# Thirty-two bytes more in a small constant: the weight tiles and all tiles behind them move in SBUF, the activations do not

## The chip, the cores and the metric

The kernel runs on one core of a Trainium2 chip. The metric is the device time of one execution in microseconds. Three runs of the kernel before took 2510.86, 2509.39 and 2510.89 us, so the median is 2510.86 us.

## The reference, cut to what matters

Two layers of a decoder trunk work on 256 tokens of width 2048. In each layer the input is projected, a gated linear recurrence (HGRN2) and a sparse attention (NSA) run on the parts, and three more projections follow:

```python
h = x @ w_in[l]                                   # 2048 -> 6704 columns
y = concat(hgrn2(...), nsa(...)) @ w_out[l]       # 2048 -> 2048
x = layer_norm(DN_ALPHA * x + y, ...)
f = conv_ffn(x, w_up[l], conv_w, conv_b, w_down[l])   # 2048 -> 2*5632 -> 2048
x = layer_norm(DN_ALPHA * x + f, ...)
```

Every number is float32, and the weights, some 430 MB, are read from HBM once.

## The kernel before, in words

**The work.** A projection is cut into units of eight pairs. A unit is one weight block `raw` of 128x1024 floats that comes in by DMA (L281). ScalarE, or GpSimd for some blocks, rounds it to a high part `whi` (L237, L235), VectorE subtracts to get the low part `wlo` (L238), and TensorE then does eight pairs of matmuls in `units` (L300): a high one (L325, or L322 for the last output tile), in which `whi` is loaded as weights and 512 columns stream past (256 tokens in a high and a low part), and a low one (L328) with `wlo` and 256 columns. Each takes its 128x128 weights from columns `128*i` of the block. In `w_up` and `w_down` eight high matmuls go first and eight low ones after them (`group=8`); in `w_out` they alternate. What streams past is `x` in `w_in` and `w_up`, `o` in `w_out` and `f` in `w_down`.

Two projections go the other way round (`tok_units`, L347): there `x` is the weights and the block streams past (L363 to L365), 512 columns at a time in the value units `w_v`, and 280 in the units `w_vg`. A `w_vg` block holds two slices of 280 columns, the second 1120 bytes behind the first; in the built program three matmuls on the first slice and three on the second take turns.

**The order of the work.** SyncE alone issues the loads, up to seven units ahead. There are five `raw` buffers, four of `whi` and four of `wlo`. A load waits until VectorE has finished with the `raw` buffer, a split waits until TensorE has finished with the part buffer.

**Where the tiles lie.** Tiles of a pool are placed one behind the other in each partition, each size rounded up to 32 bytes. The pool of constants comes first (`setup`, L167, and `load_consts`, L180), then the pool of the weights, then those of the layer. The diff touches `lbt`, a scratch tile of eight numbers in each of six rows (L217), used once at the start. The built program of before has these starts, in bytes of a partition:

| tile | start | past a multiple of 64 |
|---|---|---|
| `x` (32768 bytes) | 16512 | 0 |
| `par` | 49280 | 0 |
| `cf32` (identity, rotation tables) | 52832 | 32 |
| `cb` | 55552 | 0 |
| `ones` | 56480 | 32 |
| `lbt`, `lb` | 57088, 57280 | 0 |
| `raw`, five of 4096 bytes | 57408 | 0 |
| `whi`, `wlo`, four of 4096 bytes each | 77888, 94272 | 0 |
| `o0` to `o7`; later `f` on the same bytes | 110720 | 0 |
| `kh`, `kl`, `v`, `hz`, `sg`, `q`, `vcmp`, P and PT tiles; `z`, `s1`, `sq`; `ch`, `ct` | 143488 on | 0 |
| `hv`, `hg` | 221024, 225120 | 32 |

The second slice of a `w_vg` block lies 1120 bytes into its tile, which is 32 past a multiple of 64. The slices of `sg` that are loaded as weights at L1132 are 240 bytes apart, so one in four of them starts on a multiple of 64.

Of the kernel before, what the change touches and what calls it, by code (L numbers as in the profile page):

```python
# [29 lines left out]
F32 = mybir.dt.float32  # L30
# [73 lines left out]
class Trunk:  # L104
# [75 lines left out]
    def load_consts(self):  # L180
        nc, cp, a = self.nc, self.cp, self.a

        def ld(name, shape, dt):
            t = self.t(cp, shape, dt, name)
            self.after(nc.sync.dma_start(t, a[name]), self.load)
            return t

        self.after(self.load_par(0), self.load)
        self.lbl = ld("lbl", [128, L, 8], F32)
        self.cf = ld("cf32", [128, 673], F32)  # L190
        self.ident32 = self.cf[:, 641:673]
        self.cb = self.t(cp, [128, 416], BF16, "cb")
        self.lm = self.t(cp, [128, 80], U8, "lm")
        raw = self.t(self.wp, [128, 1024], F32, "raw", bufs=RAW_BUFS)
        self.after(nc.sync.dma_start(raw[:, :496], a["masks"]), self.load)
        nc.vector.tensor_copy(self.cb, raw[:, :416])
        nc.vector.tensor_copy(self.lm, raw[:, 416:496])
        self.ident = self.cf[:, 0:128]
        self.rc = self.cf[:, 128:384]
        self.rs = self.cf[:, 384:640]  # L200
        self.any = self.cf[:, 640:641]
        self.identb = self.cb[:, 0:128]
        self.caus = self.cb[:, 144:400]
        self.mask0 = self.cb[:, 128:416]
        self.ones = self.t(cp, [128, 128], F32, "ones")
        nc.gpsimd.memset(self.ones, 1.0 / D)
        self.eps = self.t(cp, [128, 3], F32, "eps")
        self.zero = self.eps[:, 2:3]
        nc.gpsimd.memset(self.zero, 0.0)
        self.warm = self.t(cp, [128, 1], F32, "warm")  # L210
        nc.gpsimd.memset(self.eps[:, 0:1], LN_EPS)
        nc.gpsimd.memset(self.eps[:, 1:2], RMS_EPS)
        self.half = self.t(cp, [128, 4], F32, "half")
        nc.gpsimd.memset(self.half, -0.5)

        v = nc.vector
        t = self.t(cp, [128, 6, 8], F32, "lbt")  # L217
        lb = self.lb = self.t(cp, [128, L, 2, 8], F32, "lb")
        v.tensor_max(t[:, 0], self.lbl[:, 0], self.lbl[:, 1])
        v.tensor_sub(t[:, 1], self.lbl[:, 0], t[:, 0])  # L220
        v.tensor_sub(t[:, 2], self.lbl[:, 1], t[:, 0])
        nc.scalar.activation(t[:, 1:3], t[:, 1:3], AF.Exp)
        v.tensor_add(t[:, 3], t[:, 1], t[:, 2])
        v.reciprocal(t[:, 3], t[:, 3])
        v.tensor_mul(t[:, 4], t[:, 1], t[:, 3])
        v.tensor_mul(t[:, 5], t[:, 2], t[:, 3])
        v.tensor_sub(lb[:, 0, 0], t[:, 4], t[:, 4])
        v.tensor_add(lb[:, 1, 0], t[:, 4], t[:, 5])
        v.tensor_sub(lb[:, 1, 0], lb[:, 1, 0], t[:, 4])
        for l in range(L):  # L230
            v.tensor_scalar(lb[:, l, 1], lb[:, l, 0], -1.0, 1.0, op0=ALU.mult, op1=ALU.add)
# [1111 lines left out]
```

## Time and profile before

| | |
|---|---|
| median of 3 runs | 2510.86 us (2509.39 to 2510.89) |
| profiled execution, its own time | 2509.09 us |
| its span | 2507.3 us |
| TensorE busy | 2451.8 us, 98% of the span |
| weight loads busy (overlap with TensorE) | 2116.0 us, 84% |
| VectorE, ScalarE, GpSimd busy | 71%, 48%, 17% |
| DMA | 436.99 MB, mean 174 GB/s |

Busy time is the union of an engine's instructions; matmuls are pipelined, so that the mean duration of one is longer than the distance between two. The profiled execution's own time is its span and 1.8 us around it.

### The profile page before, as it was taken

What the parts mean: (1) busy time and instruction counts of PE and PEld (TensorE: products, weight loads), DVE (VectorE), ACT (ScalarE), POOL (GpSimd) and SP (SyncE); (2) the same over time, 40 slices, a digit from 0 to 9 for tenths busy, and PEclk for the clock granted to TensorE, in tenths of its full rate; (3) what the DMA queues carried; (4) which work ended last, traced back from release to release, by engine and by line L of the source; (5) the groups of instructions that cost most, each with busy time, mean ns of one, the idle gap of its engine ahead of it and who ended that gap; (6) DMA issues with size and microseconds to landing.
All of it is one profiled execution on the core that took longest, in us unless ns stands there. A gap on an engine that the chain in (4) does not pass through costs nothing.

```text
span 2507.3 us, 41290 instructions
## 1 busy us (share of the span) xinstructions
PE 2451.8 (98%) x15993; PEld 2116.0 (84%) x15993; DVE 1780.8 (71%) x2705; ACT 1196.0 (48%) x2189; POOL 428.0 (17%) x403
## 2 busy tenths in 40 slices
PE   8999999999999999999989999999999999999997
PEld 7788877888888888888878888788888888888887
DVE  7767876787777777555597678766977777775554
ACT  4144425465555555334331444354655555553443
POOL 0444551300000000001014445513000000000011
PEclk9999999999999999999999999999999999999999
DMA  6644343556666555566546443445556565566562
GB/s 236 213 155 142 119 145 124 184 163 193 192 193 190 190 192 192 187 193 193 160 155 204 159 135 124 139 134 177 174 190 192 192 191 189 192 187 197 181 201 101
DMA packets 122884, 436.99 MB, mean 174 GB/s; under 512 B 13760, under 2 KB 14528, under 8 KB 122688
## 3 DMA queue, kind: packets, MB, share of 16 engines
q1 hardware_dynamic: 122688, 434.35, 54.0%
q8 instruction: 126, 2.06, 0.3%
q14 instruction: 70, 0.57, 0.1%
HBM read 432.20 MB, written 2.10 MB: 173 GB/s over the span
## 4 chain that ended last, share of the span: by engine, by line
PE 86%; DVE 8%; issue 2%; POOL 1%; ACT 1%; DMA 1%; SPq 0%; ACTq 0%; POOLq 0%; DVEq 0%
PE pj L325 49%; PE pj L328 26%; DVE wlo L238 3%; PE pj L322 1%; PE t L325 1%; DVE rope L400 1%; PE pj L365 1%; PE pj L364 1%; PE pj L363 1%; PE h L657 1%; DVE sg L447 1%; PE s L592 1%; POOL whi L235 1%; DMA raw<-w_in 1%; PE s L513 1%
## 5 line engine op out<-in xcount | busy, mean ns | idle before, releaser
L238 DVE TENSOR_TENSOR wlo<-raw,whi 128x1024 fp32r<-128x1024 f32 (+2 forms) x819 | 1019.3, 1246 | 534.9 <-ACT whi L237 447.0
L325 PE MATMUL pj<-x,whi 128*128 128x512 f32 x3904 | 1117.6, 395 | 8.5 <-ACT whi L237 4.6
L237 ACT ACTIVATE whi<-raw 128x1024 fp32r<-128x1024 f32 (+2 forms) x631 | 661.9, 1049 | 788.8 <-PE pj L325 598.3
L325 PEld LDWEIGHTS pj<-x,whi 128*128 128x128 f32 x3904 | 709.0, 188 | 139.7 <-ACT whi L237 4.6
L328 PE MATMUL pj<-x,wlo 128*128 128x256 f32 x3904 | 715.6, 281 | 2.6 <-DVE wlo L238 2.5
L328 PEld LDWEIGHTS pj<-x,wlo 128*128 128x128 f32 x3904 | 592.2, 188 | 38.1 <-DVE wlo L238 4.0
L325 PE MATMUL pj<-f,whi 128*128 128x512 f32 x1320 | 329.7, 392 | 0.0
L235 POOL TENSOR_SCALAR whi<-raw 128x1024 fp32r<-128x1024 f32 (+1 forms) x188 | 218.1, 1162 | 329.3 <-PE pj L325 122.9
L325 PEld LDWEIGHTS pj<-f,whi 128*128 128x128 f32 x1320 | 235.9, 188 | 40.6
L828 POOL TENSOR_TENSOR s<-z 128x512 f32<-128x512 f32 x4 | 6.8, 1706 | 1179.3 <-DVE z L825 1179.3
L328 PEld LDWEIGHTS pj<-f,wlo 128*128 128x128 f32 x1408 | 188.0, 188 | 13.6
L328 PE MATMUL pj<-f,wlo 128*128 128x256 f32 x1408 | 192.9, 278 | 0.0
L1000 DVE SCALAR_TENSOR_TENSOR ct<-ch,par,ct 128x255 f32<-128x255 f32 (+1 forms) x352 | 168.0, 481 | 5.6
L325 PE MATMUL pj<-o,whi 128*128 128x512 f32 x480 | 169.9, 396 | 1.9 <-DVE o L600 1.9
L328 PE MATMUL pj<-o,wlo 128*128 128x256 f32 x512 | 144.1, 283 | 0.0
L325 PEld LDWEIGHTS pj<-o,whi 128*128 128x128 f32 x480 | 90.1, 188 | 23.8 <-DVE o L600 2.4
L998 ACT ACTIVATE ct<-ch,par 128x256 f32<-128x256 f32 x176 | 103.0, 588 | 0.0
L328 PEld LDWEIGHTS pj<-o,wlo 128*128 128x128 f32 x512 | 96.2, 188 | 0.4
L364 PE MATMUL pj<-wlo,x 128*128 128x280 f32 (+1 forms) x256 | 90.9, 356 | 4.9 <-DVE wlo L238 4.8
L363 PE MATMUL pj<-whi,x 128*128 128x280 f32 (+1 forms) x256 | 89.7, 357 | 2.7 <-POOL whi L235 2.7
L365 PE MATMUL pj<-whi,x 128*128 128x280 f32 (+1 forms) x256 | 90.5, 356 | 0.0
L375 DVE TENSOR_TENSOR ch<-pj,ch 128x256 f32<-128x256 f32 x170 | 70.9, 418 | 3.0 <-ACT ch L374 3.0
(248 smaller groups left out, 2244.8 us busy)
## 6 DMA issues: line engine op xcount, KB each, us to landing
raw<-w_up SPq DMA_DIRECT2D x352, 512.0 KB, 4.3
raw<-w_down SPq DMA_DIRECT2D x176, 512.0 KB, 4.1
raw<-w_in SPq DMA_DIRECT2D x158, 512.0 KB, 3.8
raw<-w_out SPq DMA_DIRECT2D x64, 512.0 KB, 3.6
raw<-w_v SPq DMA_DIRECT2D x32, 512.0 KB, 3.8
raw<-w_vg SPq DMA_DIRECT2D x32, 280.0 KB, 3.0
raw<-w_c SPq DMA_DIRECT2D x16, 512.0 KB, 3.6
out<-z SPq DMA_DIRECT2D x3, 512.0 KB, 2.6
```

Of the source, the lines that this page charges most:

```text
L235: self.nc.gpsimd.tensor_scalar(hi, raw, 1.0, 0.0, op0=ALU.mult, op1=ALU.add)
L237: self.nc.scalar.activation(hi, raw, AF.Copy)
L238: return self.nc.vector.tensor_sub(lo, raw, hi.bitcast(F32))
L322: mm(out[:, 0], hi[:, o], x[:, p], start=k == 0 and p == 0, stop=False, skip_group_check=True)
L325: mm(out, hi[:, o], x, start=k == 0, stop=False, skip_group_check=True)
L328: mm(st[c][:, 0], lo[:, 128 * i:128 * i + 128], act(k)[:, 0], start=False, stop=k == nk - 1, skip_group_check=True)
L363: mm(st[tt], xh, wh, start=first, stop=False, skip_group_check=True)
L364: mm(st[tt], xh, wl, start=False, stop=False, skip_group_check=True)
L365: mm(st[tt], xl, wh, start=False, stop=kt == KT - 1, skip_group_check=True)
L375: self.nc.vector.tensor_add(out, ps[:, 0], out)
L998: act(t[:, c], h[:, c], AF.Identity, scale=w[2], bias=w[3])
L1000: v.scalar_tensor_tensor(t[:, c, s:], h[:, c, :S - s], w[n], t[:, c, s:], op0=ALU.mult, op1=ALU.add)
```

## The change

The scratch tile `lbt` gets a seventh row, which nothing reads or writes. It is 32 bytes of each partition. Whatever is placed behind it (`lb`, the weight tiles, and all tiles of the layers) starts 32 bytes later. `x`, `par`, `cf32`, `cb` and `ones` lie ahead of it and stay.

```diff
         v = nc.vector
-        t = self.t(cp, [128, 6, 8], F32, "lbt")
+        t = self.t(cp, [128, 7, 8], F32, "lbt")
         lb = self.lb = self.t(cp, [128, L, 2, 8], F32, "lb")
```

No instruction, wait, buffer or transfer is added or taken away. Behind the change `raw`, `whi`, `wlo`, `o`, `f` and the other tiles of the table that were on a multiple of 64 bytes are 32 past one, and `hv` and `hg` are on one.

## Rows read from the trace of the kernel before

**Rows 1.** The page: busy us, share of the span and instructions of each engine.
```profile
PE 2451.8 (98%) x15993; PEld 2116.0 (84%) x15993; DVE 1780.8 (71%) x2705; ACT 1196.0 (48%) x2189; POOL 428.0 (17%) x403
```

**Rows 2.** Windows: length, busy PE, PEld, DVE, ACT, POOL, clock, DMA share, GB/s.
```profile
512.00:1230.00 718.00, 717.65 (x4172) 631.81 (x4170) 497.13 (x698) 382.06 (x549) 22.54 (x14) 1.00 0.60 190
```

**Rows 3.** Groups by line and form, PE: shape, count, busy us, mean ns, idle before.
```profile
L325 PE MATMUL pj<-x,whi 128*128 128x512 f32 x3904 | 1117.6, 395 | 8.5 <-ACT whi L237 4.6 <-POOL whi L235 2.8 <-DVE x L975 1.0
L328 PE MATMUL pj<-x,wlo 128*128 128x256 f32 x3904 | 715.6, 281 | 2.6 <-DVE wlo L238 2.5
L325 PE MATMUL pj<-f,whi 128*128 128x512 f32 x1320 | 329.7, 392 | 0.0
L328 PE MATMUL pj<-f,wlo 128*128 128x256 f32 x1408 | 192.9, 278 | 0.0
L325 PE MATMUL pj<-o,whi 128*128 128x512 f32 x480 | 169.9, 396 | 1.9 <-DVE o L600 1.9
L328 PE MATMUL pj<-o,wlo 128*128 128x256 f32 x512 | 144.1, 283 | 0.0
...
L363 PE MATMUL pj<-whi,x 128*128 128x512 f32 x128 | 52.8, 413 | 0.0
```

**Rows 4.** Load of cf32: timeline of SP (start, duration); issue groups (KB, us to landing).
```profile
20.16 0.47 SPq L185 DMA_DIRECT2D cf<-cf  x1
...
cf<-cf SPq DMA_DIRECT2D x1, 336.5 KB, 7.6
```

**Rows 5.** Windows ahead of that landing and around it: columns as in rows 2.
```profile
24.00:27.20 3.20, 3.20 (x20) 2.81 (x19) 1.55 (x4) 1.25 (x2) 0.00 (x0) 1.00 1.03 411
27.20:30.00 2.80, 2.80 (x18) 2.43 (x17) 2.08 (x9) 1.84 (x3) 0.00 (x0) 1.00 0.85 339
```

**Rows 6.** Waits, longest in total: us, times, longest us.
```profile
ACT whi L237 <- PE pj L325: 598.3, 449, 3.1
```

**Rows 7.** Groups by line and form, DVE and ACT: ch, hz and hg.
```profile
L375 DVE TENSOR_TENSOR ch<-pj,ch 128x256 f32<-128x256 f32 x170 | 70.9, 418 | 3.0 <-ACT ch L374 3.0
...
L375 DVE TENSOR_TENSOR hg<-pj,hg 128x256 f32<-128x256 f32 x16 | 6.7, 420 | 7.9 <-ACT hg L374 7.6
...
L374 ACT ACTIVATE hz<-pj 128x256 f32<-128x256 f32 x36 | 13.9, 387 | 57.0 <-PE pj L328 56.9
...
L374 ACT ACTIVATE hg<-pj 128x256 f32<-128x256 f32 x16 | 6.2, 389 | 23.9 <-PE pj L328 23.9
```

**Rows 8.** Timeline, PE, units w_vg: start, duration; every third matmul.
```profile
41.03 0.29 PE L363 MATMUL pj<-whi,x 128*128 128x280 f32 x1
...
41.42 0.29 PE L363 MATMUL pj<-whi,x 128*128 128x280 f32 x1
...
41.80 0.29 PE L363 MATMUL pj<-whi,x 128*128 128x280 f32 x1
```

**Rows 9.** Timeline, PE: pairs of matmuls, weights vcmp (L589) and ones (L791).
```profile
160.96 0.59 PE L589 MATMUL s<-rope,vcmp 128*128 128x256 f32 x2
...
465.94 0.59 PE L791 MATMUL s<-s,ones 128*128 128x256 f32 x2
```

**Rows 10.** Timeline, PEld: weight loads in a row, of sq (L873), then ones (L867).
```profile
502.66 0.53 PEld L873 LDWEIGHTS t<-ones,sq 128*128 128x128 f32 x4
503.11 0.30 PEld L867 LDWEIGHTS s<-z,ones 128*128 128x128 f32 x2
```

**Rows 11.** Line L1132, weight loads of slices of sg: shortest, median, longest ns.
```profile
L1132 PEld LDWEIGHTS h<-raw,sg x128: 129/133/223, 55.9 to 1343.9; 128*60 128x60 f32 x128
```

**Rows 12.** Timeline, PE, in w_down: runs of eight high and eight low matmuls.
```profile
2279.47 2.00 PE L325 MATMUL pj<-f,whi 128*128 128x512 f32 x8
2281.30 1.07 PE L328 MATMUL pj<-f,wlo 128*128 128x256 f32 x8
2282.21 1.99 PE L325 MATMUL pj<-f,whi 128*128 128x512 f32 x8
2284.04 1.11 PE L328 MATMUL pj<-f,wlo 128*128 128x256 f32 x8
```

## The prediction

> **What bounds the kernel now.** I read the page's busy times first: TensorE is busy for 98% of the span [rows 1]. A share over the whole span says little about a stage, so the second view is the busy time by window. In the first layer's `w_up` and `w_down` (from 512 to 1230 us) TensorE is idle for 0.35 of 718 us at a granted clock of 1.00, no other engine is full, and DMA is at 0.60 [rows 2]; the second layer repeats it. There a nanosecond on each matmul is paid in full, while a slower VectorE, ScalarE or transfer would be hidden at first. The third view is the groups by form. A high matmul of 512 columns lasts 395 ns with `x` streaming, 392 with `f`, 396 with `o`; a low one of 256 columns lasts 281, 278 and 283 [rows 3]. These lengths are not distances: in the timeline the next run starts 1.83 us after a run of eight high ones and 0.91 us after one of eight low ones, or 0.229 and 0.114 us for each matmul [rows 12]. The kernel is bound by how fast TensorE streams columns and, in the low runs, perhaps by how fast it loads weights.
>
> **The change, part by part.** It issues nothing and removes nothing; no queue is passed, no wait is added. Only addresses differ, so the sum is over users of an address that goes from a multiple of 64 bytes to 32 past one. For each I look for something in the old trace that already starts 32 past.
>
> *The transfers into `raw`.* `cf32` starts 96 bytes past a multiple of 512 (52832 = 103 x 512 + 96). `raw` will start at 57440 = 112 x 512 + 96, the same remainder. The load of `cf32` is issued at 20.16 us and lands 7.6 us later, at 27.8 [rows 4]. In the window ahead of that the DMA moves 411 GB/s at a share of 1.03, or 399 for a share of one; in the window from 27.2 on, 339 at 0.85, again 399 [rows 5]. The 336.5 KB are a quarter of what 411 GB/s bring in 3.2 us (1315 KB), so had they taken twice the time, the rate for a share of one would have been about a fifth lower. I take nothing. The cover is that a split waits for TensorE to release its part buffer, 598.3 us in 449 waits [rows 6]: blocks lie ready before they are needed. From above: a transfer that took half as long again would lift the share from 0.60 [rows 2] to 0.90, which still doesn't bind.
>
> *The splits and other vector work.* The sum in L375 has 418 ns on `ch`, aligned, and 420 on `hg`, 32 past; the copy in L374 has 387 on `hz` and 389 on `hg` [rows 7]. I take nothing. If the 2 ns were real they would lie beside TensorE and off the path; the cover is again the waits of the splits [rows 6], and were it gone, a unit of 2.7 us (1.83 + 0.91) would grow by 2 ns.
>
> *The streams that move.* `x` stays, so the 2 x 3904 matmuls on it keep their stream. `f`, `o` and the blocks of `tok_units` shift: 1320 + 1408 + 480 + 512, and 3 x 128 in the value units (L364 and L365 are like L363), 4104 matmuls [rows 3]. The units `w_vg` are the measurement: three matmuls on an aligned slice, three on one 32 past, in turn. The starts are 41.03, 41.42 and 41.80: 0.39 us for three aligned, 0.38 for three shifted [rows 8]. From below the price is nothing: the 0.01 us less is the resolution of the timeline. From above, a start in mid-piece may cost as much as the 8 columns in 32 bytes: (395 - 281) / 256 = 0.445 ns a column [rows 3], 3.6 ns a matmul, 4104 x 3.6 = 14.6 us; if both ends of a piece of 64 bytes were paid, 16 columns and 29.2 us. I take nothing, since these rows have the same kind of number and the same stream. They don't settle it: 280 columns are 17 and a half pieces of 64 bytes, so that either start leaves one half piece, while 512 columns are whole pieces only when aligned.
>
> *The weight loads that move.* All `whi` and `wlo` loads start 32 past. The high ones hide under 0.229 us of stream. The low ones, 3904 + 1408 + 512 = 5824 [rows 3], have little cover: loads in a row without a long stream are (0.53 - 0.19) / 3 = 0.113 us apart, 0.19 being the length of one, and a short low run has (1.07 - 0.28) / 7 = 0.113 us between matmuls [rows 10, 12]. `ones` is loaded from 32 past: two such loads in a row take 0.30, or 0.11 apart, no more than those of aligned `sq` [rows 10]. A pair of matmuls takes 0.59 us with `ones` as with aligned `vcmp` [rows 9]. I take nothing. The bound from above is L1132: the shortest load of a slice of `sg` is 129 ns, the median 133, and three slices in four are not aligned [rows 11]. Four ns on each low load would be 23.3 us, on those in the shorter sets of eight alone half of it.
>
> The sum is 0 us against the profiled execution's 2509.09 us (span 2507.3 and 1.8 around it), which is 1.8 under the median of 2510.86. I forecast the median, **2510.9 us**.
>
> **One page of the Trainium skill.** "SBUF — State Buffer", section "Specifications (TRN2)", says that SBUF has lines of 16 bytes and that each crossing to a new line costs. By it a shift of 32 bytes moves every stream and load by two whole lines and the number of crossings stays, so the sum would be 0, where the upper bounds from the rows give 29.2 and 23.3 us. The trace agrees for streams of 280 columns (0.39 and 0.38 us [rows 8]); no run here shows it for 512.
>
> **The rivals.**
>
> *Slower, by weight loads.* A load that starts 32 past takes longer, and the low runs become bound by loading. It decides from the point where a load needs more than the 0.113 us of a short low run. For it: there is no slack in that number, and L1132 shows a spread of 4 ns. Against: `ones` [rows 9, 10]. These are plain float32 loads, which are not quite the same as those of the split weights. Price: 11.6 us if only the shorter sets of eight suffer (2522), 23.3 at most (2534).
>
> *Slower, by streams.* `f`, `o` and the value blocks pay for a broken first piece: 2510.9 + 14.6 = 2525.5, or + 29.2 = 2540. For it: the stage that streams `f` has no idle time [rows 2]. Against: the streams of `w_vg` [rows 8]. `w_up` would not change, which tells it from the first.
>
> *A shifted rhythm.* Low runs alternate between 1.07 and 1.11 us although each does the same work [rows 12]. Something falls in step every second run. In two layers `w_up` has 2 x 88 x 16 = 2816 low matmuls and `w_down` 2 x 16 x 44 = 1408, so there are 528 runs of eight, 264 of each sort. Should the shift put all into the short step, the gain is 264 x 0.04 = 10.6 us (2500); all into the long one, the loss is as much (2521.5). For it: what sets the step isn't seen, and addresses may be part of it. Against: `x` and `f`, at different addresses, have the same lengths.
>
> That the change does nothing at all, because the placement rounds to more than 32 bytes, is excluded: `lm` with 80 bytes at 56384 is followed by `ones` at 56480.
>
> **How the numbers follow.** A measurement of this kernel can tell about 0.2% from no change, 5.0 us. No change within that has a chance of 0.50. Slower loads get 0.17 and slower streams 0.16, since the rows are against both, but neither row has the exact operation. The rhythm gets 0.12 for faster and 0.05 for slower. So faster is 0.12, same 0.50, slower 0.38. The range goes from 2500, where the whole rhythm gains, to 2540, the upper bound of the streams; what lies outside, loads and streams together or an effect not thought of, I put at under 0.2. The likeliest case alone is 2506 to 2516.
>
> **What would show it.** If right, the profile after has low runs in `w_down` of 1.07 and 1.11 us in turn, high runs of about 2.00, `f` at 392 and 278 ns, and VectorE splits, DMA share and idle times as before. Slower loads would show in low runs of both `w_up` and `w_down`, above 1.11 us, with high runs kept. Slower streams would show in `w_down`, `w_out` and the value units alone. A new rhythm would be low runs all of one length. If the transfers were wrong after all, TensorE would have idle time in the long stages, released by a DMA; if the splits were, by VectorE or ScalarE.

## The result, and the profile after

The changed kernel takes 2530.38 us (median of four runs, 2527.49 to 2531.33), the kernel before 2510.88 us beside it (four runs, 2509.39 to 2513.19). The ratio is 1.0073 with a 95% interval from 1.0061 to 1.0086: slower by 0.7%. The profiled execution took 2530.93 us with a span of 2529.1, which is 21.8 us more than the 2507.3 of before. Both kernels issue the same instructions in the same order.

First the page of the changed kernel: its busy times and its transfers of the longest stage.

```profile
PE 2464.8 (97%) x15993; PEld 2121.7 (84%) x15993; DVE 1782.4 (70%) x2705; ACT 1195.6 (47%) x2189; POOL 423.4 (17%) x403
...
raw<-w_up SPq DMA_DIRECT2D x352, 512.0 KB, 4.0
```

Against [rows 1], the engines' busy times hardly move. The window of [rows 2], busy time by engine, granted clock and DMA share, from 512 to 1230 us:

```profile
512.00:1230.00 718.00, 717.66 (x4118) 625.04 (x4118) 494.93 (x699) 378.89 (x548) 22.58 (x14) 1.00 0.59 188
```

TensorE has no idle time here, its granted clock is 1.00 as before, the DMA share is 0.59 instead of 0.60. So no wait was added in this stretch; TensorE itself goes through its work more slowly. The groups by form say on which matmuls to look (shape, count, busy us and mean ns, idle before):

```profile
L325 PE MATMUL pj<-x,whi 128*128 128x512 f32 x3904 | 1125.5, 397 | 10.8 <-POOL whi L235 5.3 <-ACT whi L237 4.5 <-DVE x L975 1.0
L325 PE MATMUL pj<-f,whi 128*128 128x512 f32 x1320 | 329.7, 392 | 0.0
L325 PE MATMUL pj<-o,whi 128*128 128x512 f32 x480 | 169.6, 396 | 1.9 <-DVE o L600 1.9
```

Beside [rows 3], `f` and `o` have kept their 392 and 396 ns to the nanosecond, and `x`, the one stream that was not moved, went from 395 to 397. A mean length says little about pipelined matmuls, so I go by starts. The next two fences are the view by tile: name of the group, count, shortest/median/longest ns, then **first and last start**. `o` begins `w_out`, `x` in these windows begins `w_up` of the first and second layer, `f` begins `w_down` (of the first layer, then of the second). Before:

```profile
L325 PE MATMUL pj<-o,whi x480: 388/397/496, 405.9 to 1743.5; 128*128 128x512 f32 x160
...
L325 PE MATMUL pj<-x,whi x1308: 388/392/473, 513.1 to 979.9; 128*128 128x512 f32 x187
...
L325 PE MATMUL pj<-f,whi x1320: 388/392/477, 998.5 to 2472.2; 128*128 128x512 f32 x189
...
L325 PE MATMUL pj<-x,whi x1352: 388/392/473, 1758.2 to 2239.7; 128*128 128x512 f32 x194
...
L325 PE MATMUL pj<-f,whi x660: 388/392/477, 2243.6 to 2472.2; 128*128 128x512 f32 x165
```

After:

```profile
L325 PE MATMUL pj<-o,whi x480: 388/397/502, 409.4 to 1758.1; 128*128 128x512 f32 x160
...
L325 PE MATMUL pj<-x,whi x1280: 389/394/467, 516.3 to 979.8; 128*128 128x512 f32 x183
...
L325 PE MATMUL pj<-f,whi x1320: 387/392/478, 1009.0 to 2494.0; 128*128 128x512 f32 x189
...
L325 PE MATMUL pj<-x,whi x1360: 389/394/472, 1772.7 to 2264.3; 128*128 128x512 f32 x195
...
L325 PE MATMUL pj<-f,whi x660: 387/392/477, 2265.4 to 2494.0; 128*128 128x512 f32 x165
```

The differences of the first starts, read down, give the delay as it grows, and so the loss of each stretch:

| up to the first matmul of | before | after | delay | gained since the row above |
|---|---|---|---|---|
| `w_out`, layer 1 | 405.9 | 409.4 | 3.5 | 3.5 (mixer) |
| `w_up`, layer 1 | 513.1 | 516.3 | 3.2 | -0.3 (`w_out`) |
| `w_down`, layer 1 | 998.5 | 1009.0 | 10.5 | **7.3 (`w_up`)** |
| `w_up`, layer 2 | 1758.2 | 1772.7 | 14.5 | 4.0 (`w_down` 1, mixer 2, `w_out` 2) |
| `w_down`, layer 2 | 2243.6 | 2265.4 | 21.8 | **7.3 (`w_up`)** |
| last high matmul of `w_down` | 2472.2 | 2494.0 | 21.8 | 0.0 (`w_down`) |

`w_up` takes 492.7 us instead of 485.4 in each layer, 14.6 of the 21.8 us. `w_down`, from its first to its last high matmul of 512 columns, takes 228.6 in both kernels. What sits in `w_up` shows in the timeline of TensorE (start, duration, runs of equal instructions). Before, in `w_up`; the first line is the first set of eight of the stage:

```profile
546.41 2.00 PE L325 MATMUL pj<-x,whi 128*128 128x512 f32 x8
...
902.05 2.00 PE L325 MATMUL pj<-x,whi 128*128 128x512 f32 x8
903.88 1.07 PE L328 MATMUL pj<-x,wlo 128*128 128x256 f32 x8
904.79 1.99 PE L325 MATMUL pj<-x,whi 128*128 128x512 f32 x8
906.62 1.11 PE L328 MATMUL pj<-x,wlo 128*128 128x256 f32 x8
907.56 2.00 PE L325 MATMUL pj<-x,whi 128*128 128x512 f32 x8
```

After, in `w_up`:

```profile
549.79 2.03 PE L325 MATMUL pj<-x,whi 128*128 128x512 f32 x8
...
902.59 2.03 PE L325 MATMUL pj<-x,whi 128*128 128x512 f32 x8
904.46 1.09 PE L328 MATMUL pj<-x,wlo 128*128 128x256 f32 x8
905.39 2.03 PE L325 MATMUL pj<-x,whi 128*128 128x512 f32 x8
907.26 1.09 PE L328 MATMUL pj<-x,wlo 128*128 128x256 f32 x8
908.19 2.03 PE L325 MATMUL pj<-x,whi 128*128 128x512 f32 x8
```

After, in `w_down`:

```profile
2301.27 2.00 PE L325 MATMUL pj<-f,whi 128*128 128x512 f32 x8
2303.10 1.07 PE L328 MATMUL pj<-f,wlo 128*128 128x256 f32 x8
2304.01 1.99 PE L325 MATMUL pj<-f,whi 128*128 128x512 f32 x8
2305.84 1.11 PE L328 MATMUL pj<-f,wlo 128*128 128x256 f32 x8
```

`w_down` is what it was, alternation and all [rows 12]. In `w_up` the alternation is gone, and a low run now starts 1.87 us after a high one where it was 1.83; the step after a low run is 0.93 where 0.91 and 0.94 took turns. Two units took 907.56 - 902.05 = 5.51 us and take 908.19 - 902.59 = 5.60. `w_up` has 176 units in a layer. The first 12, for the first six output tiles, go two pairs at a time (`min(group, 2)` in `units`); they take 546.41 - 513.1 = 33.3 us before and 549.79 - 516.3 = 33.5 after. The other 164 go in sets of eight, which makes 82 of these steps of two: 82 x 0.09 = 7.4 us, against 7.3 - 0.2 = 7.1 from the starts.

The rest lies ahead of `w_out`. There TensorE does wait more (waits of the first 409 us: us in all, times, longest). Before:

```profile
PE s L513 <- ACT o L517: 0.9, 2, 0.6
```

After:

```profile
PE s L513 <- ACT o L517: 2.6, 2, 1.9
```

All waits of this stretch together go from 20.1 to 24.2 us, enough for the 3.5 us of the first layer. Which operation became late first is left open.

### The profile page after: what moved, and what is told of

Same layout as the page of the kernel before. It is cut to its first block, busy times and chain, and to the rows that moved or that the text cites. A ratio compares the mean times of both kernels' runs of the same rounds, so it can differ in the third digit from the quotient of the medians.

```text
span 2529.1 us, 41290 instructions
## 1 busy us (share of the span) xinstructions
PE 2464.8 (97%) x15993; PEld 2121.7 (84%) x15993; DVE 1782.4 (70%) x2705; ACT 1195.6 (47%) x2189; POOL 423.4 (17%) x403
## 4 chain that ended last, share of the span: by engine, by line
PE 86%; DVE 8%; issue 2%; DMA 1%; POOL 1%; ACT 1%; SPq 0%; ACTq 0%; POOLq 0%; DVEq 0%
PE pj L325 49%; PE pj L328 25%; DVE wlo L238 3%; DMA raw<-w_in 1%; PE pj L322 1%; PE t L325 1%; PE pj L365 1%; PE pj L364 1%; PE pj L363 1%; PE h L657 1%; DVE rope L400 1%; POOL whi L235 1%; DVE sg L447 1%; PE s L592 1%; PE s L513 1%
## 5 line engine op out<-in xcount | busy, mean ns | idle before, releaser
L238 DVE TENSOR_TENSOR wlo<-raw,whi 128x1024 fp32r<-128x1024 f32 (+2 forms) x819 | 1023.2, 1251 | 558.3 <-ACT whi L237 462.2
L325 PE MATMUL pj<-x,whi 128*128 128x512 f32 x3904 | 1125.5, 397 | 10.8 <-POOL whi L235 5.3
L325 PEld LDWEIGHTS pj<-x,whi 128*128 128x128 f32 x3904 | 709.7, 189 | 147.4 <-POOL whi L235 5.8
L328 PE MATMUL pj<-x,wlo 128*128 128x256 f32 x3904 | 719.0, 282 | 2.7 <-DVE wlo L238 2.7
L328 PEld LDWEIGHTS pj<-x,wlo 128*128 128x128 f32 x3904 | 595.8, 189 | 41.6 <-DVE wlo L238 4.1
L325 PE MATMUL pj<-f,whi 128*128 128x512 f32 x1320 | 329.7, 392 | 0.0
L325 PEld LDWEIGHTS pj<-f,whi 128*128 128x128 f32 x1320 | 235.9, 188 | 40.6
L328 PEld LDWEIGHTS pj<-f,wlo 128*128 128x128 f32 x1408 | 188.0, 188 | 13.6
L328 PE MATMUL pj<-f,wlo 128*128 128x256 f32 x1408 | 193.0, 278 | 0.0
L325 PE MATMUL pj<-o,whi 128*128 128x512 f32 x480 | 169.6, 396 | 1.9 <-DVE o L600 1.9
L328 PE MATMUL pj<-o,wlo 128*128 128x256 f32 x512 | 144.0, 283 | 0.0
L325 PEld LDWEIGHTS pj<-o,whi 128*128 128x128 f32 x480 | 90.1, 188 | 23.7 <-DVE o L600 2.4
L328 PEld LDWEIGHTS pj<-o,wlo 128*128 128x128 f32 x512 | 96.1, 188 | 0.4
```

What stands on the lines that cost most here:

```text
L238: return self.nc.vector.tensor_sub(lo, raw, hi.bitcast(F32))
L325: mm(out, hi[:, o], x, start=k == 0, stop=False, skip_group_check=True)
L328: mm(st[c][:, 0], lo[:, 128 * i:128 * i + 128], act(k)[:, 0], start=False, stop=k == nk - 1, skip_group_check=True)
```

## The experiments

What distinguishes `w_up` from `w_down` in the new kernel? The weight tiles moved by 32 bytes, and `f` and `o` with them, but `x` did not. I call **distance** the start of a weight block less the start of the stream that runs past it, modulo 128 bytes, by the addresses of the tiles. Before, `x` lay at 0 of 128, `whi` and `wlo` at 64, `f` and `o` at 0: the distance was 64 everywhere. After, the weights lie at 96, `f` and `o` at 32, `x` still at 0: 64 for `f` and `o`, and 96 for `x` alone. In the expectations, theory D says that the distance counts (at first modulo 64), theory A that the absolute start of the weight tiles does. The modulus is a way of writing: that the distance repeats every 128 bytes is not shown. In every stage of sets that kept its old time, the distance is the old one modulo 512 as well.

The table has all twelve kernels; times in us. The kernels of the first four rows were timed in rounds beside 2511.94 (13 runs, 2509.91 to 2515.4) and have intervals; the others are one run each, beside 2510.24, the last beside 2511.65. `w_up` goes from its first matmul to the first of `w_down` in the first layer (both starts in brackets), 485.4 before and 492.7 after; in every kernel the second layer repeats the first within 0.2 us. The kernels e5, e6, e9 and e10 also move `o` by 64 and `f` by 128 bytes.

| kernel | distance `x` | distance `f`, `o` | time | against before | `w_up` |
|---|---|---|---|---|---|
| e1_all_moved | 64 | 64 | 2510.89 | 0.9994 [0.9985, 1.0003] | 485.5 (513.3 to 998.8) |
| e2_x_alone | 32 | 64 | 2536.83 | 1.0090 [1.0073, 1.0106] | 497.6 (514.9 to 1012.5) |
| e3_f_o_back | 96 | 32 | 2539.97 | 1.0105 [1.0090, 1.0120] | 492.7 (516.8 to 1009.5) |
| e4_64_bytes | 0 | 64 | 2523.21 | 1.0038 [1.0023, 1.0053] | 491.7 (514.4 to 1006.1) |
| e5_whi_alone | `whi` all four, `wlo` 64 | `f` the same; `o`: `whi` all four, `wlo` 0 | 2530.37 | +20.1 | 492.9 (514.7 to 1007.6) |
| e6_wlo_alone | `whi` 64, `wlo` all four | `f` the same; `o`: `whi` 0, `wlo` all four | 2532.89 | +22.7 | 491.0 (516.7 to 1007.7) |
| e7_distance_80 | 80 | 64 | 2529.5 | +19.3 | 494.0 (514.5 to 1008.5) |
| e8_distance_48 | 48 | 64 | 2525.3 | +15.1 | 493.0 (512.7 to 1005.7) |
| e9_whi_96 | `whi` 96, `wlo` 64 | `f` the same; `o`: `whi` 32, `wlo` 0 | 2539.52 | +29.3 | 494.1 (515.7 to 1009.8) |
| e10_wlo_96 | `whi` 64, `wlo` 96 | `f` the same; `o`: `whi` 0, `wlo` 32 | 2522.98 | +12.7 | 488.9 (513.2 to 1002.1) |
| e11_distance_68 | 68 | 64 | 2510.64 | +0.4 | 487.3 (511.5 to 998.8) |
| e12_alternating_up | 96, high and low in turn | 64 | 2517.62 | +6.0 | 488.3 (515.0 to 1003.3) |

**Everything 32 bytes on.** From the kernel before, a tile of 32 bytes is put ahead of `x`, so that `x` moves like all the rest. The addresses of the weights are those of the changed kernel.

```diff
+        self.ahead = self.t(self.cp, [128, 8], F32, "ahead")
         self.x = self.t(self.cp, [128, KT, 2, S], F32R, "x")
```

> A tile of 32 bytes ahead of x: everything moves by 32 bytes, x as well, so that x and the weight tiles are again the same distance past a multiple of 64, but all of them 32 past one. Theory D (the distance between the stream and the weights counts, modulo 64): the time is that of before, 2511 us, and w_up of a layer takes 485 us as before. Theory A (where the weight tiles start counts by itself): 2530 us as with the change, w_up 493 us.

Timeline in `w_up` (L326 and L329 are L325 and L328, one line down):

```profile
902.30 2.00 PE L326 MATMUL pj<-x,whi 128*128 128x512 f32 x8
904.14 1.07 PE L329 MATMUL pj<-x,wlo 128*128 128x256 f32 x8
905.04 1.99 PE L326 MATMUL pj<-x,whi 128*128 128x512 f32 x8
906.87 1.11 PE L329 MATMUL pj<-x,wlo 128*128 128x256 f32 x8
```

The old lengths, the old alternation and the old time are back, `w_up` at 485.5. The place of the weights alone is therefore not the cause. The mixer is back as well: the waits of L514 (which is L513, one line down) on ScalarE's `o` are 0.9 us again, and all waits of the first 409 us 20.5.

**`x` alone moved.** The weights, `f` and `o` keep the places of the kernel before; `x` begins 32 bytes into a longer tile, and a scratch tile gives up as many bytes (its rows are used again). The constants between the two move by 64 bytes. Against the kernel before:

```diff
-        self.x = self.t(self.cp, [128, KT, 2, S], F32R, "x")
+        self.x = self.t(self.cp, [128, KT * 2 * S + 16], F32R, "x")[:, 8:8 + KT * 2 * S].rearrange(
+            "p (k a t) -> p k a t", k=KT, a=2)
...
-        t = self.t(cp, [128, 6, 8], F32, "lbt")
+        t = self.t(cp, [128, 4, 8], F32, "lbt")
```

> Only x moves by 32 bytes; weights, o, f and the tiles of the mixers stay where they were before (lbt reuses two rows to make room, par and the constants move by 64). Theory D: w_up takes 493 us in each layer as with the change, w_down 252 us as before, so at least 2525 us. Theory A: 2511 us, w_up 485 us. What the mixers do shows whether their 4 us a layer come from x against the weights or from other tiles.

Timeline in `w_up`:

```profile
902.23 2.03 PE L326 MATMUL pj<-x,whi 128*128 128x512 f32 x8
904.10 1.12 PE L329 MATMUL pj<-x,wlo 128*128 128x256 f32 x8
905.06 2.03 PE L326 MATMUL pj<-x,whi 128*128 128x512 f32 x8
```

With every weight where it was, `w_up` takes 497.6 us, 12.2 more than before: theory A falls. Nor is it the place of `x` by itself, which is the same in e1. Distance 32 is worse than 96, so the two sides of 64 are not alike. High sets take the same 1.87 us as in the change, low ones 0.96 instead of 0.93.

**`f` and `o` back in place.** From the changed kernel, the two pads ahead of `o` and `f` grow by 32 bytes, so that their distance to the weights is 32.

```diff
-        self.pad = self.t(mo, [128, 16], F32, "pad")
+        self.pad = self.t(mo, [128, 24], F32, "pad")
...
-            self.pad = self.t(fp, [128, 16], F32, "pad")
+            self.pad = self.t(fp, [128, 24], F32, "pad")
```

> The changed kernel with 32 bytes more in the two pad tiles: weights and x as with the change, but o, f and everything behind them back on multiples of 64. Theory D: w_up stays at 493 us, and w_down, whose stream is now 32 bytes off its weights, becomes slower: 1408 pairs in two layers at some 5 ns, 3.7 us a layer, so about 256 us a layer in place of 252, and about 2537 us in all. Theory A: w_down stays at 252 us, 2530 us in all.

`w_down` of the second layer in the view by tile, then its timeline:

```profile
L325 PE MATMUL pj<-f,whi x660: 388/394/484, 2269.0 to 2503.2; 128*128 128x512 f32 x165
```

```profile
2300.06 2.03 PE L325 MATMUL pj<-f,whi 128*128 128x512 f32 x8
2301.93 1.12 PE L328 MATMUL pj<-f,wlo 128*128 128x256 f32 x8
2302.89 2.03 PE L325 MATMUL pj<-f,whi 128*128 128x512 f32 x8
```

The loss was brought into `w_down`, which takes 2503.2 - 2269.0 = 234.2 us instead of 228.6, while `w_up` keeps its 492.7. The lengths are those of `w_up` in e2 (2.03, 1.12, steps of 1.87 and 0.96): the same distance of 32 gives the same sets, with another stream and weights at another place. By this measure `w_down` has 82.5 high sets, about half of the 164 of `w_up`, and 5.6 us is about half of 12.2. `w_out`, whose stream `o` is at 32 here as well, does its matmuls in turn and loses nothing: from its first matmul to the first of `w_up` it takes 106.7 us, and 107.2 before.

**64 bytes instead of 32.** The scratch tile has eight rows; the distance of `x` is 0. Against the kernel before:

```diff
-        t = self.t(cp, [128, 6, 8], F32, "lbt")
+        t = self.t(cp, [128, 8, 8], F32, "lbt")
```

> lbt gets two rows more in place of one: everything behind it moves by 64 bytes. Theory D: as before, 2511 us, w_up 485 us, since the distance modulo 64 is the same. If the distance counts modulo 128, w_up differs from 485 us, to either side, and w_down does not.

Timeline in `w_up`:

```profile
899.93 2.00 PE L325 MATMUL pj<-x,whi 128*128 128x512 f32 x8
901.78 1.12 PE L328 MATMUL pj<-x,wlo 128*128 128x256 f32 x8
902.73 2.00 PE L325 MATMUL pj<-x,whi 128*128 128x512 f32 x8
```

Here I had guessed that the distance counts modulo 64. It doesn't: at 0 `w_up` costs 6.3 us, and the high sets take 1.85 us and the low ones 0.95. What repeats, if anything does, repeats at 128 or more.

**Which of the two loads?** Two kernels were to move `whi` or `wlo` alone, by a tile of 1032 floats of which the last 1024 are used, and without the pad ahead of `o`. The edit of e5:

```diff
+    def part(self, tag):
+        n = 8 if tag == "whi" else 0
+        return self.t(self.wp, [128, 1024 + n], F32R, tag, bufs=PART_BUFS)[:, n:]
...
-        self.pad = self.t(mo, [128, 16], F32, "pad")
```

> The kernel before with 32 bytes ahead of the block in each whi buffer alone: whi is 96 bytes past a multiple of 128, wlo, raw, x and f stay as before modulo 128 (o goes to 64, by 64). Theory D, applied to each load by itself: sets of eight high matmuls take 233 ns a matmul as with the change, in w_up and w_down, and the low ones stay at 116, so w_up takes about 491 us (176 sets by 8 x 4.4 ns more) and w_down some 3 us more than 252. If the effect belongs to the low loads, w_up stays at about 485 to 487 us.

> The same with wlo alone 32 bytes on. Theory D for each load by itself: high matmuls at 229 ns, low ones at 116.7 in place of 115.8, w_up about 486.7 us. If the two kinds of load work on each other (the stream of one set ends on loads of the other), w_up takes more than that, up to 493.

The edit was flawed: with 4128 bytes from buffer to buffer, the four buffers lie at four places modulo 128, so each kernel mixes four distances. They cost 20.1 and 22.7 us, 7.5 and 5.6 of it in each `w_up`, and can't be set against one expectation. One thing shows in the timeline of e5, from 903 to 912 us: the steps after the low runs are 0.92 to 0.95 us, whichever place `whi` has, and none returns to 0.91.

> The kernel before with a gap of 32 bytes ahead of the whi buffers and of 96 ahead of the wlo buffers: all four whi buffers are 96 past x modulo 128, all four wlo buffers 64 past it, f stays at 0. (In e5 and e6 the four buffers came to four different places, since each was 32 bytes longer.) If a load counts by its own distance, high matmuls take 233 ns, low ones 116, and w_up some 491 us. If a set carries its state over to the next one, as sets with both parts at 64 did in e5 (233 ns for high ones in place of 229), the low ones change as well and the sum of 491 is not met.

> The same with the wlo buffers alone at 96 past x modulo 128, whi at 64. By its own distance: high ones 229 ns, low ones 116.7, w_up about 486.7 us. With a state carried over: high ones above 229 although nothing about their own loads is changed, and w_up well above 487 us.

These put all buffers of a kind at one distance, with gap tiles ahead of the buffers. The edit of e10; e9 has gaps of 8 and 24 floats, no pad ahead of `o` and the old one ahead of `f`.

```diff
+            for tag, gap in (("whi", 0), ("wlo", 8)):
+                if n == 1 and gap:
+                    self.t(self.wp, [128, gap], F32, "gap" + tag)
+                pair.append(self.t(self.wp, [128, 1024], F32R, tag, bufs=PART_BUFS))
...
-        self.pad = self.t(mo, [128, 16], F32, "pad")
+        self.pad = self.t(mo, [128, 24], F32, "pad")
...
-            self.pad = self.t(fp, [128, 16], F32, "pad")
+            self.pad = self.t(fp, [128, 40], F32, "pad")
```

In e9 `w_up` takes 494.1 us, more than with both kinds at 96 (492.7; I had expected about 491). But its gaps move `wlo` by 128 bytes as well, so it moves `whi` alone only if 128 bytes do not count.

In e10 `whi`, `raw` and `x` are exactly where they were before, and `wlo` alone is 32 bytes on. `w_up` takes 488.9 us, 3.5 more than before. Its timeline (L331 is L325, L334 is L328):

```profile
902.15 2.01 PE L331 MATMUL pj<-x,whi 128*128 128x512 f32 x8
904.00 1.09 PE L334 MATMUL pj<-x,wlo 128*128 128x256 f32 x8
904.94 2.00 PE L331 MATMUL pj<-x,whi 128*128 128x512 f32 x8
906.77 1.10 PE L334 MATMUL pj<-x,wlo 128*128 128x256 f32 x8
```

The high runs start the low ones 1.85 and 1.83 us later in turn, where it was 1.83 each time, although neither their weights nor their stream has moved. So a set pays a little for the place of the sets around it. Whether that is their distance to the stream or to `whi`, no run separates. In `w_down` of e10:

```profile
2301.62 2.03 PE L331 MATMUL pj<-f,whi 128*128 128x512 f32 x8
2303.49 1.10 PE L334 MATMUL pj<-f,wlo 128*128 128x256 f32 x8
```

`whi` and `f` are 64 apart modulo 128 here too, but `f` has moved on by 128 bytes, and the step is 1.87 us. `w_down` takes 232.3 us, 3.7 more than before, for about half the sets of `w_up`. The same distances modulo 128 thus have about twice the price per set, which speaks against a repeat every 128 bytes. So e5, e6 and e9, which rely on one, do not show what each kind of matmul pays alone.

**How sharp is the 64?** From e2, with a longer tile for `x` and another first column, at 12, 20 and 15 floats; everything behind `x` moves by 64 bytes. The line of e11:

```diff
+        self.x = self.t(self.cp, [128, KT * 2 * S + 32], F32R, "x")[:, 15:15 + KT * 2 * S].rearrange(
+            "p (k a t) -> p k a t", k=KT, a=2)
```

> x alone is placed so that the weight blocks start 80 bytes past it modulo 128 (64 before, 96 with the change); f and o keep their 64. If the cost grows steadily with the distance from 64, w_up takes about 489 us, half of the way from 485.4 to 492.7. If it comes in steps of 32 bytes, it is 485 or 493. If 64 is not the best place, it is under 485.

> As the run before, with 48 bytes modulo 128 in place of 64. Steady growth: about 491 us for w_up, half of the way from 485.4 to the 497.6 measured at 32. Steps of 32 bytes: 485 or 498. Under 485 if 64 is not the best place.

> x alone placed so that both parts are 68 bytes past it modulo 128, four bytes from the best place so far. If the good place is as wide as a piece of 16 bytes or more, w_up stays at 485.4 us; if it is one exact distance, w_up takes 490 us or more as at 48 and 80.

At 80 and at 48 `w_up` takes 494.0 and 493.0 us: 16 bytes to either side cost 8.6 and 7.6, more than 32 bytes do on the one side. At 68, 4 bytes off, it is 487.3, between the alternatives that I had set. Timeline of e11:

```profile
901.88 2.00 PE L326 MATMUL pj<-x,whi 128*128 128x512 f32 x8
903.72 1.09 PE L329 MATMUL pj<-x,wlo 128*128 128x256 f32 x8
904.65 2.00 PE L326 MATMUL pj<-x,whi 128*128 128x512 f32 x8
```

All low runs are 1.09 us long, as in the change, and 0.93 us from the next, but the high ones step by 1.84 us and not by 1.87. So the lost alternation, which the changed kernel shows too, is not itself the greater part of the loss. The kernel's 2510.64 us equal the 2510.24 beside it although its two `w_up` lose 3.9 us: against the profile of before it gains 1.6 us ahead of the first `w_up` (511.5 and not 513.1) and 0.8 between the first `w_down` and the second `w_up`, and the rest, 1.5, is no more than single runs of a kernel differ.

**Sets or pairs?** From the changed kernel, `w_up` does its high and low matmuls in turn, as `w_out` does. The same matmuls run at the same distance of 96.

```diff
-                        pre={(0, 0): pre_up}, wide=OUTER, group=8)
+                        pre={(0, 0): pre_up}, wide=OUTER, group=1)
```

> The changed kernel with high and low matmuls of w_up in turn (as in w_in and w_out) in place of sets of eight. In the units of w_in, which alternate, the mean pair took 350.1 ns before (231.9 + 118.2) and 348.1 with the change (230.3 + 117.8), no more. If the cost of the distance 96 belongs to sets of one kind of load and stream, w_up takes 1408 x 0.348 = 490 us, under the 492.7 of the changed kernel. If the distance costs every pair 5 ns whatever the order, it takes 1408 x 0.355 = 500 us.

```profile
900.03 0.39 PE L325 MATMUL pj<-x,whi 128*128 128x512 f32 x1
900.25 0.28 PE L328 MATMUL pj<-x,wlo 128*128 128x256 f32 x1
```

`w_up` takes 488.3 us, 4.4 less than with sets at that distance, and the kernel is 12.8 us faster than the changed one was (2530.38). How much of the 2.9 us over 485.4 belongs to the distance is not shown, since no kernel has the whole of `w_up` in turn at 64. The nearest thing is the first 12 units, two pairs at a time: 33.3 us before, at 64, are 0.347 us for each of the 96 pairs, and 488.3 us are 0.347 for each of the 1408 pairs of e12, at 96. These 12 units paid 0.2 of the 7.3 us of the change; at 32, in e2, they took 34.0 (514.9 to 548.9). With `w_out` in e3, at 32 and no slower, this says that at 96 nearly all of the price lies in the sets of eight of a kind, and not in each matmul. No kernel of the twelve beats the kernel before by what can be told apart.

## Why the prediction was wrong

The forecast of 2510.9 us, no change with 0.50, missed by 19.5 us. The range of 2500 to 2540 holds the time, but by luck: its upper part was priced for slower loads in the low runs and for slower moved streams, and neither came about.

**The step that failed** is in the streams: "`x` stays, so the 2 x 3904 matmuls on it keep their stream". They kept the stream and lost their distance to the weights. The whole sum went over users of an address one by one, and asked of each alone whether a start 32 past something costs more. None does: with everything 32 bytes on, e1 takes 0.9994 of the time. Two thirds of the loss, 14.6 of 21.8 us, were in the stretch whose stream the sum had set aside as unmoved, `w_up`, by pairing `x` at its old place with weights at their new one.

**The witnesses could not see it.** `w_vg` at 0.39 and 0.38 us [rows 8] is in the changed kernel at 0.38 to 0.39 too. By the measure of the experiments it even had both distances: with `x` at 0 as the weights, its two slices start at 64 and at 32 modulo 128, so that the distances are 64 and 96, in turn. It shows no difference. What sets it apart from `w_up` is that it does three matmuls of 280 columns on a slice, and not sets of eight; the row was read rightly and stood for too much. `ones`, `cf32` and `hg` [rows 4, 5, 7, 9, 10] each tell of one address. A row can stand for another operation only in what it shares with it, and none of these had sets of eight matmuls of a kind at two distances.

**What held.** The transfers: issue to landing 4.0 us for `w_up`, DMA share 0.59. The splits: L238 takes 1251 ns on the mean of all its shapes, 1246 before, and holds nothing up in the long stages, where TensorE is idle for 718 - 717.66 = 0.34 us. The streams `f` and `o` at 392 and 396 ns, and `w_down` at 228.6 us. These steps were costed at nothing and cost nothing.

**The rivals.** *By streams* falls at once: `w_down` unchanged, `w_up` changed, the reverse of what it needed. *By weight loads* named the low runs of both stages above 1.11 us with high runs kept; the low runs are 1.09, `w_down` is unchanged, and it is the high runs that grew. Its size (2522 to 2534) fits, its mechanism does not. The lower price was also summed wrongly: half of all 5824 low loads gives 11.6 us, but the shorter sets of eight have at most 264 x 8 = 2112 of them, or 8.4 us. *A shifted rhythm* comes nearest. It said "low runs all of one length", which `w_up` shows, and "addresses may be part of it". It was priced on the low runs alone, 264 x 0.04 = 10.6 us at most, for both stages and with 0.05 on the slower side. Measured: 328 high runs of `w_up` (two layers, 164 each) at 0.04 us more, 13.1 us, and 164 x 0.01 = 1.6 us on the low ones (0.91 and 0.94 became 0.93 twice). The 7.2 us outside `w_up`, nearly all in the mixers, had no place in any of the three; they vanish in e1 as well, but through which wait the places of the tiles work on them is not shown.

**The page.** The sum of nothing was also what the prediction took from the Trainium skill, "SBUF — State Buffer", section "Specifications (TRN2)", with its lines of 16 bytes. The runs differ. Distances of 48 and 80 are each one whole line from 64 and cost 7.6 and 8.6 us in one `w_up`, while 68, no whole number of lines away, costs 1.9. The measurement decides: for these sets, the number of lines that one access crosses is not what sets the time.

**What stays open.** That the distance decides in sets of eight is shown by moving either side (e1, e2, e3) and by the times at seven distances. In e1 to e4 `raw` moves with the parts, but e10 leaves `raw` and still costs 3.5 us in `w_up`. Why the old distance is best, with what period it returns, and whether two reads collide or a rhythm between loads and streams locks in, is not shown: no view shows the reads themselves. That high sets pay when only the low ones have moved (e10) speaks for a rhythm, but doesn't prove it.

## What to carry to other kernels

Where TensorE has no idle time and does sets of matmuls of a kind, the place of a weight tile relative to the tile that streams past it is a parameter of the kernel, worth up to 1% here (e2 and e3): a harmless new tile ahead of one of the two can cost it. Keep the two moving together, as e1 does, or put a pad between them and measure a few distances; here the old distance, 64 modulo 128 bytes, was the best of seven, from 32 bytes less to 64 more. Try the matmuls in turn as well: at 96 that order was better by 4.4 us in `w_up`. And when an edit moves some tiles and leaves others, list the pairs of operands whose relation changes, not only the operands that move.

## What was not expected of the hardware

- The time of a set of eight high and eight low matmuls depends on the distance between weights and stream: `w_up` takes 485.4 us at 64, 487.3 at 68, 491.7 at 0, 492.7 at 96, 493.0 at 48, 494.0 at 80 and 497.6 at 32, at a granted clock of 1.00 in that stage in all these profiles and with TensorE never idle from 520 to 980 us.
- The absolute place of the same tiles, 32 bytes on, is worth nothing (0.9994 [0.9985, 1.0003]).
- The same matmuls at distance 96 cost 4.4 us less in `w_up` when high and low ones alternate than in sets of eight.
- High sets whose weights and stream have not moved step by 1.85 and 1.83 us in turn, and not by 1.83, when the low sets between them have moved by 32 bytes (`w_up` of e10).
- 128 bytes more between `f` and the weights are not without effect: `w_down` of e10 pays 3.7 us for distances that cost 3.5 us in `w_up`, with about half the sets.
